# The closing sums of the modulation groups traced with a lower priority

## The chip, the cores and the metric

The kernel runs on one core of a Trainium2 chip. The metric is the device time of one execution in microseconds (us). Before the change three runs took 2878.17, 2879.86 and 2882.39 us, the median is 2879.86 us.

## The reference

The reference computes two layers of a backbone over 512 latent and 256 context tokens of width 1024, in float32. Each layer has a SwiGLU feed-forward half step (ffn1), a mixer of four head groups, and a second half step (ffn2). What the change touches is only the modulations: nine vectors of 1024 numbers for each layer, for the latent tokens (from c) and for the context tokens (from c_ctx), which shift and scale the inputs of each step and gate its output.

```
def ada_mods(s, w, b, dt):
    m = (s @ w.astype(jnp.float32) + b.astype(jnp.float32)).astype(dt)
    m = m.reshape(m.shape[0], N_MOD, D_MODEL)
    return [m[:, k, None, :] for k in range(N_MOD)]

def ffn_half(h, g, w_i, w_o, shift, scale, gate):
    y = modulate(rms_norm(h, g), shift, scale)
    a, b = jnp.split(y @ w_i, 2, axis=-1)
    return h + FFN_RES * gate * ((jax.nn.silu(a) * b) @ w_o)
```

Here s is the SiLU of c or c_ctx (two rows), and w has 1024 rows and 9216 columns for each layer.

## The kernel before

The tokens lie along the free axis, the features on the 128 partitions. A product of float32 operands is made of three TensorE products of parts of 12 bits: a weight tile `wr` from DRAM is split into `wh` (a copy on ACT, L378) and the rest `wl` (a subtraction on DVE, L379), and the input is kept as a pair of such parts, `g`. A column tile of a feed-forward input is 8 row blocks x 3 products x 2 pieces of the tokens (258 and 510 columns, their form is named 128x258 and 128x512), 48 matmuls at L389 into one PSUM tile `pi`. The tiles go in pairs: tile a (for the SiLU), then tile b (the factor). The PSUM pool `psb` that they and the output products `po` share has two buffers, so the next pair's tile a needs the buffer that this pair's tile a leaves. It is left when DVE has copied two shift columns (L448, `bc`) and multiplied the tile by the tokens' norm factors (L449, `z<-pi,R`). For tile b DVE does L453 and L455.

Under these products lies the work of the modulations that later steps need, in `ada_steps`: 32 groups of 512 columns (14 of layer 0 in its ffn1, 9 of layer 1 in layer 0's ffn2, 9 more in layer 1's ffn1). A group has two loads `wa` of 1 MB (L248) and 16 operations of DVE on them (2 at L254, which begin the two sums `acc`, and 14 at L256, which add to them). Then `done()` closes the group: four matmuls by a column of ones add `acc` over the partitions (L263, output `pa`; the profile shows each as two records), ACT copies the sums (`arow`, L265), two transposes (L268, output `pt`) turn them, and DVE adds them and the bias into the modulations (L238). The two `acc` are buffers of the pool `small` under the tag "sq", of which there are two in all: the next group's L254 can begin only when this group's L263 has read its `acc`. In the feed-forward input the loads `wr` and `wa` take turns in the same buffers (tag "wraw").

Each engine executes its own queue in order. The order is set when the program is built: the scheduler of the tile context takes, for each engine, from the instructions whose inputs a simulated time line has ready the one of the highest priority, and the priority is the place in which it was traced, unless the code raises or lowers it (`tc.high_priority(offset)`; a negative offset puts the instructions that many places later). The hooks, among them the two steps of each group, are traced between the column tiles. L1559 and L1564 are matmuls of the S5 coefficients, traced as hooks too; L281 makes a gate from the modulations, L495 adds an output product to the residual; L1438, L1460 to L1462 are DVE operations for S5.

Of the kernel before, what the change touches and what calls it, by code (L numbers as in the profile page):

```python
# [30 lines left out]
FINAL_AT = 2  # L31
SUMS_AT = 1


class Net:
# [63 lines left out]
    def setup_rest(self):  # L99
        """what the first tiles' first products don't need"""  # L100
        nc = self.nc
        for f in self.ada_first(0, 4, "l" * 12 + "z" * 4):
            f()
        for j in range(NT):
            self.hg_shift(j, 0, 0)
        self.rms_factor(TT)
        self.load_rpb()
        self.load_vectors(0, self.REST)
        for part in (self.FIRST, self.REST):
            self.load_vectors(1, part)  # L110
        for t, s in ((self.cos, "k_cos"), (self.sin, "k_sin"), (self.perm, "k_perm"), (self.bones, "k_bones")):
            nc.sync.dma_start(t, self.A[s])

    def load_rpb(self):
        """the neighbourhood's biases with something to read before and after them"""
        nc = self.nc
        m = 2 * 4 * 15 * 31
        self.rpb = self.dram.tile([m + 128], F32, name="rpb")
        z = self.const.tile([1, 64], F32, name="zrow")
        nc.vector.memset(z, 0.0)  # L120
        nc.sync.dma_start(self.rpb[0:64].unsqueeze(0), z)
        nc.sync.dma_start(self.rpb[64 + m:128 + m].unsqueeze(0), z)
        nc.sync.dma_start(self.rpb[64:64 + m].unsqueeze(0), self.A["na_rpb"].rearrange("l h a b -> (l h a b)").unsqueeze(0))
# [5 lines left out]
    def load_vectors(self, l, names=None):  # L129
        """rows to columns; of a layer's rows the first ones or those after them"""  # L130
        nc, A = self.nc, self.A
        pk = self.small.tile([P, TT], F32, name=self.nm("pack"), tag="sq", bufs=2)[:, :P]
        if l < 2:
            q = nc.scalar if l == 0 and names == self.FIRST else nc.sync
# [29 lines left out]
    def load_rows(self, t, b):  # L164
        """128 tokens' half"""
        raw = self.t("g")
        src = self.A["x"][0, t * P:(t + 1) * P, :] if t < 4 else self.A["ctx"][0, (t - 4) * P:(t - 3) * P, :]
        self.nc.sync.dma_start(raw[:, :512], src[:, b * 512:(b + 1) * 512])
        return raw
# [14 lines left out]
    def park(self):  # L184
        """the residual, to DRAM"""
        self.hd = self.dram.tile([NT, P, TT], F32, name=self.nm("hd"))
        for j in range(NT):
            self.nc.sync.dma_start(self.hd[j], self.h[j][:, :TT])
# [6 lines left out]
    def ada_first(self, q0, groups, tags):  # L195
        """two loads of 512 columns of the first layer's modulations, from 512 * q0 on, and products on TensorE, `groups`
        of them at a time: closures for two row blocks each, loads and products on their own if asked for"""
# [34 lines left out]
    def ada_add(self, l, c, parts):  # L232
        """parts, [128, q, b, r], and the bias"""
# [6 lines left out]
    def ada_steps(self, l, q, ring=None):  # L240
        """two closures for 512 columns of a layer's modulations: products on VectorE, their sum over the partitions on
        TensorE"""
# [3 lines left out]
        def rows(k0):  # L246
# [10 lines left out]
            if k0:  # L257
                done()
# [35 lines left out]
    def hg_tile(self, j, l, mi, gs, nt):  # L294
        """`mi` None: the shifts come later, and the squares are there"""
# [23 lines left out]
    def exp_small(self, pool, out, x):  # L319
        """exp of a few numbers, to float32's accuracy, on VectorE"""  # L320
# [16 lines left out]
    def rsqrt(self, r, src, scale):  # L337
        """(src * scale + eps) ** -0.5 of a few numbers: a guess from the exponent, three steps of Newton's"""
# [56 lines left out]
    def in_tile(self, w, nt):  # L395
        """[128, 1024]: columns 254, 255 the shifts' products, from 256 on the tokens'"""
        ps = self.psb.tile([P, 1024], F32, name=self.nm("pi"), tag="psb")
        self.mm(self.in_chunks(ps, nt), w, self.hgx, NT)
        return ps
# [4 lines left out]
    def in_pair(self, wa, wb, nt, late):  # L404
        """two of them; what needs the shifts, made by `late`, comes last"""
# [9 lines left out]
    def ffn(self, l, w_in, w_out, gate, nt, finish, hooks=(), late=None, ring=None):  # L415
        """`gate` is called when it is first needed; `hooks` are traced one list by one between the column tiles;
        `late` is called before the first product that needs the shifts,
        `ring` is for the output's weights if given"""
# [102 lines left out]
    def split_kept(self, raw, kn, j):  # L521
        """the two parts of a column tile's weights, to be kept"""
# [38 lines left out]
    def sums(self, hf, c):  # L561
        """tokens' factors; the second half's last squares come on their own"""
# [34 lines left out]
class Mixer:  # L597
    """One layer's four head groups. Tokens: latent 0..511, context 512..767."""
# [40 lines left out]
    def scratch(self, name):  # L639
        """a pool for what comes next in the place of the last one"""  # L640
# [6 lines left out]
    # column tile, whether it has the context's tokens in any case, where it goes, order of tokens  # L647
# [4 lines left out]
    def beside(self):  # L652
        """what is traced after which column tile"""
# [13 lines left out]
    def evac(self, ps, nt, tag, way):  # L667
        """tokens * R + bias; the latent ones column by column if `way` says so"""
# [16 lines left out]
    def split(self, src, nt, tag="l", slow=False):  # L685
        """a high part and what is left"""
# [10 lines left out]
    def lru(self):  # L697
        """states of both directions, added; the gates' sigmoids as 0.5 + 0.5 tanh(x / 2)"""
# [70 lines left out]
    def softplus_neg(self, o, lam):  # L769
        """8 * softplus(-lam), [128, 4]"""  # L770
# [25 lines left out]
    def softmax(self, p, s, acc, bias=None, r=-1.0):  # L796
        """exp(x - max) and its sums; r * (s + bias) is -x"""
# [7 lines left out]
    def transposed(self, dst, blocks, scalar):  # L805
        """128-column blocks, transposed, side by side in dst"""
# [7 lines left out]
    def attention(self):  # L814
        """all units, each one's stages one after the other's; a group's operands are made ahead of it"""
# [20 lines left out]
    def group(self, units, done):  # L836
        """units in pairs of heads; `done` with (o, factors), [64 of two heads, queries] in PSUM, behind the last; a
        unit: scores, probabilities' parts to multiply with what"""
# [35 lines left out]
    def factors(self, sm, m):  # L874
        """1 / sums [queries, m] as [64 of two heads, queries]"""
# [10 lines left out]
    def ctx_units(self, qs, ks, vs, y, r=lambda qi, hh: -1.0):  # L886
        """two heads' context queries over the context's keys"""
# [16 lines left out]
    def gqa_norm(self):  # L904
        """each token's factors of its two heads, the queries', negative, for the scores; v token by token"""
# [27 lines left out]
    def gqa_scale(self):  # L933
        """the keys' factors"""
# [8 lines left out]
    def gqa_turn(self):  # L943
        """positions' rotations"""
# [9 lines left out]
    def stack_q(self, src, nt, scale=1.0, tag="g"):  # L954
        """[hi; lo] of each of a tile's two heads"""
# [10 lines left out]
    def stack_k(self, src, hh, tag="g"):  # L966
        """[hi; hi] and [lo; lo] of one of a tile's two heads"""
# [9 lines left out]
    def stack_ks(self, src):  # L977
        """the same of both heads"""
# [49 lines left out]
    def na_gather(self, head):  # L1028
        """[queries (c, r), (row, column) of keys in a band] of the head's biases"""
# [8 lines left out]
    def na_bias(self, gs, v):  # L1038
        """two heads' masked biases [queries (c, r), keys (c, r)], and zeros for the context's keys"""
# [67 lines left out]
    def s5_in(self):  # L1107
        """u as [group, h, 7 - s, chunk], chunks ctx | lat | ctx, in DRAM"""
# [134 lines left out]
def mixed(units, more):  # L1243
    """pairs of `more` behind some pairs of the units"""
# [11 lines left out]
def by_columns(ap, way):  # L1256
    """[128, row, column] of tokens that lie column by column, from the first on or from the last"""
# [4 lines left out]
def tables():  # L1262
    """what depends on shapes alone"""
# [36 lines left out]
class S5Coef:  # L1300
    """Coefficients of a layer's S5 scans in chunks of 8 tokens, parked in DRAM.
    [128 (re|im, state), 32 (direction, group)] throughout, but for the tables of rotations:
    [128 (direction, state), 16 groups, 95]."""

    def __init__(self, net, l):
# [3 lines left out]
        # by (direction, pair of groups): the two products' weights; cos, sin, decay  # L1309
# [5 lines left out]
    def steps(self):  # L1315
        """closures, traced one after the other; pools open with the first and close with the last"""
# [28 lines left out]
    def base(self):  # L1345
# [39 lines left out]
        # (a - 1) / lambda  # L1385
# [18 lines left out]
        # powers 0..8 of a; the imaginary parts as [-; +]  # L1404
# [22 lines left out]
    def load(self, d):  # L1427
        """one direction's b, [re; im] and [im; re], and c; the skip's weights, as diagonals"""
# [18 lines left out]
    def bc(self, d):  # L1447
        """one direction's b and c with the discretization's factor and with signs"""
# [22 lines left out]
    def tables(self):  # L1471
        """cos and sin of the chunks' angles, by doubling"""
# [22 lines left out]
        for g in range(0, 16, 4):  # L1495
# [4 lines left out]
            m = 1  # L1500
# [23 lines left out]
    def weights(self, g0):  # L1524
        """two groups of one direction"""
# [47 lines left out]
    def toeplitz(self):  # L1573
        """[group, h, (t - s + 7, h')] of both directions"""
# [19 lines left out]
def spread(hooks, steps, first=0):  # L1594
    """evenly over the column tiles from the `first` on, but the last of each group"""
# [71 lines left out]
```

## Time and profile before

| | before |
|---|---|
| runs, us | 2878.17, 2879.86, 2882.39 (median 2879.86) |
| span of the profiled execution | 2877.7 us |
| TensorE busy | 2819.1 us (98%) |
| VectorE busy | 1742.3 us (61%) |
| ScalarE busy | 906.5 us (32%) |
| GpSimd busy | 757.7 us (26%) |
| DVE on L256, 448 instructions | 358.6 us, 849 ns each |

The profile gives the span of the profiled execution, from its first to its last instruction; the median of the runs is 2.2 us longer, which is taken for what lies around the span. A row of a time line is a start, a duration, the engine, the source line, the operation with output and inputs by the program's names, and in brackets how long the engine stood idle before it and what it waited for. Rows with x2 or x4 put several instructions together.

### The profile page before, as it was taken

How to read it: one execution, taken by the hardware profiler on the slowest of the kernel's cores; microseconds unless marked ns; L12 is line 12 of the kernel's file. 1: busy time of each engine (PE TensorE's matmuls, PEld its weight loads, DVE VectorE, ACT ScalarE, POOL GpSimd, SP SyncE). 2: the span in 40 equal slices, each digit the busy share in tenths (PEclk: the TensorE clock that was granted, in tenths of full speed). 3: DMA queues.
4: the chain of work that ended last, by engine and by line, in shares of the span. 5: the costliest groups of instructions: out<-in, count | busy, mean ns of one | idle time of the engine just before them, and what ended most of it. 6: DMA issues, size and time to landing. Idle time of an engine off the chain costs nothing.

```text
span 2877.7 us, 43478 instructions
## 1 busy us (share of the span) xinstructions
PE 2819.1 (98%) x17293; PEld 2437.7 (85%) x17293; DVE 1742.3 (61%) x3178; ACT 906.5 (32%) x1478; POOL 757.7 (26%) x957
## 2 busy tenths in 40 slices
PE   7999999999999999999999999999999999999998
PEld 4888888888877888888888888888888887899998
DVE  6868577676857566363634766465466876444445
ACT  4212121235546422112123321222224645322223
POOL 2822233221323311000001176332312434201001
PEclk9999999999999999999999999999999999999999
DMA  6445324353323333222311335233254343232231
GB/s 227 134 108 167 112 96 141 123 185 118 115 62 74 103 115 99 87 96 95 107 54 54 118 101 142 80 123 106 74 168 145 118 106 89 79 96 83 88 96 52
DMA packets 295901, 312.13 MB, mean 108 GB/s; under 512 B 58991, under 2 KB 243202, under 8 KB 295698
## 3 DMA queue, kind: packets, MB, share of 16 engines
q1 hardware_dynamic: 266990, 293.97, 31.8%
q0 software_dynamic: 5664, 12.59, 1.9%
q10 hardware_dynamic: 23044, 2.78, 0.7%
q8 instruction: 137, 2.24, 0.3%
q14 instruction: 66, 0.54, 0.1%
HBM read 276.09 MB, written 29.02 MB: 106 GB/s over the span
## 4 chain that ended last, share of the span: by engine, by line
PE 88%; DVE 6%; DMA 2%; ACT 2%; issue 1%; POOL 0%; SPq 0%; ACTq 0%; DVEq 0%; POOLq 0%
PE pi L389 51%; PE po L389 23%; PE po L1236 4%; DVE acc L256 2%; PE po L862 2%; PE pt L810 2%; DMA wa<-in_w_ada_dram 1%; PE ps L793 1%; PE pa L263 1%; DVE wl L379 1%; PE ps L794 1%; DMA l<-in_w_ada_dram 1%; PE pl L734 1%; DVE z L455 0%; PE pa L215 0%
## 5 line engine op out<-in xcount | busy, mean ns | idle before, releaser
L389 PE MATMUL pi<-g,wh 128*128 128x258 f32 (+2 forms) x6656 | 1408.7, 330 | 8.4 <-ACT wh L378 2.6
L389 PEld LDWEIGHTS pi<-g,wh 128*128 128x128 f32 x6656 | 1101.4, 191 | 132.2 <-issue 15.0
L389 PE MATMUL pi<-g,wl 128*128 128x258 f32 (+2 forms) x3328 | 828.1, 329 | 0.7 <-DVE wl L379 0.7
L378 ACT CAST wh<-wr 128x1024 fp32r<-128x1024 f32 (+3 forms) x380 | 338.2, 890 | 1397.4 <-PE pi L389 674.8
L389 PEld LDWEIGHTS pi<-g,wl 128*128 128x128 f32 x3328 | 607.4, 191 | 60.6 <-issue 2.5
L389 PE MATMUL po<-l,wh 128*128 128x512 f32 (+1 forms) x2464 | 566.1, 344 | 0.9 <-DVE e L495 0.8
L389 PEld LDWEIGHTS po<-l,wh 128*128 128x128 f32 x2464 | 387.9, 188 | 63.9 <-issue 3.9
L459 POOL TENSOR_TENSOR l<-z,l 128x768 fp32r<-128x768 f32 (+1 forms) x88 | 159.1, 1808 | 1061.4 <-ACT l L458 955.4
L379 DVE TENSOR_TENSOR wl<-wr,wh 128x1024 fp32r<-128x1024 f32 (+3 forms) x380 | 407.0, 1071 | 50.3 <-ACT wh L378 47.5
L256 DVE SCALAR_TENSOR_TENSOR acc<-wa,s,acc 128x512 f32<-128x512 f32 x448 | 358.6, 849 | 39.4 <-DMA wa<-in_w_ada_dram 38.6
L495 DVE SCALAR_TENSOR_TENSOR e<-po,gt,e 128x512 f32<-128x512 f32 (+1 forms) x296 | 176.2, 631 | 307.4 <-PE po L389 250.7
L389 PE MATMUL po<-l,wl 128*128 128x512 f32 (+1 forms) x1232 | 337.5, 343 | 1.0 <-DVE wl L379 1.0
L453 DVE TENSOR_TENSOR z<-pi,R 128x768 f32<-128x768 f32 (+2 forms) x91 | 78.4, 865 | 301.3 <-PE pi L389 301.3
L389 PEld LDWEIGHTS po<-l,wl 128*128 128x128 f32 x1232 | 194.5, 188 | 32.6 <-DVE wl L379 2.0
L448 DVE COPY bc<-pi 128x2 f32<-128x2 f32 x88 | 13.7, 156 | 189.4 <-PE pi L389 189.4
L458 ACT CAST l<-z 128x768 fp32r<-128x768 f32 (+1 forms) x88 | 68.8, 782 | 160.5 <-DVE z L455 160.5
L1545 POOL TENSOR_TENSOR ww<-AR,BB 128x256 f32<-128x256 f32 x32 | 25.9, 808 | 341.4 <-PE pw L1564 309.5
L455 DVE SCALAR_TENSOR_TENSOR z<-z,pi,z 128x512 f32<-128x512 f32 (+1 forms) x154 | 107.1, 730 | 5.5 <-ACT z L451 0.7
L317 POOL TENSOR_TENSOR ssq<-ssq,sq 128x768 f32<-128x768 f32 (+1 forms) x35 | 67.5, 1929 | 161.0 <-ACT sq L316 161.0
L451 ACT ACTIVATE z<-z,bc 128x512 f32<-128x512 f32 (+1 forms) x154 | 90.0, 625 | 62.7 <-DVE z L449 51.3
L449 DVE TENSOR_TENSOR z<-pi,R 128x768 f32<-128x768 f32 (+1 forms) x88 | 77.5, 880 | 3.7 <-ACT R L366 3.7
L1236 PE MATMUL po<-l,wh 128*128 128x512 f32 (+1 forms) x264 | 71.9, 356 | 0.0
(349 smaller groups left out, 2632.0 us busy)
## 6 DMA issues: line engine op xcount, KB each, us to landing
wr<-in_w_ffn_in_dram SPq DMA_DIRECT2D x88, 1024.0 KB
wa<-in_w_ada_dram SPq DMA_DIRECT2D x64, 1024.0 KB
wr<-in_w_ffn_out_dram SPq DMA_DIRECT2D x48, 512.0 KB
wr<-in_w_ffn_out_dram SPq DMA_DIRECT2D x32, 640.0 KB
wr<-in_w_in_dram SPq DMA_DIRECT2D x16, 1024.0 KB
W<-s5w SPq DMA_DIRECT2D x32, 256.0 KB
wr<-in_w_out_dram SPq DMA_DIRECT2D x8, 1024.0 KB
l<-in_w_ada_dram SPq DMA_DIRECT2D x24, 256.0 KB
```

Source lines behind the costliest of these rows:

```text
L256: nc.vector.scalar_tensor_tensor(acc[r], raw[:, k], s, acc[r], ALU.mult, ALU.add)
L378: nc.scalar.copy(hi[:, :kn], raw[:, :, o:o + P])
L379: nc.vector.tensor_sub(lo[:, :kn], raw[:, :, o:o + P], hi[:, :kn].bitcast(F32))
L389: nc.tensor.matmul(dst, lhsT=wt[:, k, :], rhs=xt[:, a:b], start=(k == 0 and i == 0), stop=(k == kn - 1 and i == 2))
L449: nc.vector.tensor_mul(ta[:, :nt], pa[:, 256:256 + nt], self.R[:, :nt])
L451: nc.scalar.activation(ta[:, a:b], ta[:, a:b], AF.Silu, bias=bc[:, i:i + 1])
L453: nc.vector.tensor_mul(tb[:, a:b], p, self.R[:, a:b])
L455: nc.vector.scalar_tensor_tensor(tb[:, a:b], tb[:, a:b], pb[:, 254 + i:255 + i], ta[:, a:b], ALU.add, ALU.mult)
L458: nc.scalar.copy(uh[:, :nt], tb[:, :nt])
L459: nc.gpsimd.tensor_sub(ul[:, :nt], tb[:, :nt], uh[:, :nt].bitcast(F32))
L495: self.nc.vector.scalar_tensor_tensor(self.h[j][:, a:b], ps[:, a:b], gate[:, j, i:i + 1], self.h[j][:, a:b], ALU.mult, ALU.add)
L1236: self.nc.tensor.matmul(dst, lhsT=wt[:, k, :], rhs=xt[:, a:b], start=(c == 0 and i == 0), stop=(c == NT - 1 and i == 2))
```

## The change

`done()`, the part that closes a group, is traced with a priority 150 places lower. Nothing else is computed in another way; the numbers of instructions are the same on every engine. (The rest of the diff empties comments.)

```
+CLOSING = 150
@@ in ada_steps, rows(k0)
             if k0:
-                done()
+                with self.tc.high_priority(offset=-CLOSING):
+                    done()
```

Lines of the changed kernel stand one or two further down: L254 becomes L255, L256 L257, L263 L265, L268 L270, L238 L239, L379 L381, L389 L391, L449 L451, L453 L455, L455 L457, L448 L450, L1559 L1561, L1564 L1566, L1567 L1569.

The first place is in layer 0's ffn2, TensorE's queue at the closing `pa_1553` with its transposes `pt_1555`. Before, it stands between the tiles of a pair: behind tile b of the pair that has just ended (`pi_1543`) and ahead of the next tile a (`pi_1560`), whose PSUM buffer is long free.

```order
L389 MATMUL pi_1543_9876<-g_1514_9647,wh_1541_9872 128x258
L389 MATMUL pi_1543_9876<-g_1514_9647,wh_1541_9872 128x512
L263 MATMUL pa_1553_9961<-acc_1550_9941,ones_80 32x256 x2
L263 MATMUL pa_1553_9961<-acc_1551_9943,ones_80 32x256 x2
L389 MATMUL pi_1560_9980<-g_1464_9168,wh_1558_9976 128x258
L389 MATMUL pi_1560_9980<-g_1464_9168,wh_1558_9976 128x512
```

Now it stands one pair later: `pi_1560` (tile a) and `pi_1563` (tile b) are ahead of it, and `pi_1574`, the next tile a, behind it.

```order
L391 MATMUL pi_1563_10033<-g_1514_9647,wh_1561_10029 128x258
L391 MATMUL pi_1563_10033<-g_1514_9647,wh_1561_10029 128x512
L265 MATMUL pa_1553_9961<-acc_1550_9941,ones_80 32x256 x2
L265 MATMUL pa_1553_9961<-acc_1551_9943,ones_80 32x256 x2
L270 MATMUL pt_1555_9968<-ident_78,z_1554_9962 128x128 x2
L391 MATMUL pi_1574_10112<-g_1464_9168,wh_1572_10108 128x258
L391 MATMUL pi_1574_10112<-g_1464_9168,wh_1572_10108 128x512
```

The 96 matmuls of a pair have moved ahead of the closing; the transposes now follow it at once.

On VectorE the same place, before: the next group's sums `acc_1570` and `acc_1571` begin while tile a runs, and the multiplication that frees `pi_1560` comes among the additions.

```order
L379 TENSOR_TENSOR wl_1559_9977<-wr_1556_9972,wh_1558_9976 128x1024
L453 TENSOR_TENSOR z_1546_9927<-pi_1543_9876,R_84 128x768
L254 TENSOR_SCALAR acc_1570_10098<-wa_1569_10096,s2_102 128x512
L254 TENSOR_SCALAR acc_1571_10100<-wa_1569_10096,s2_102 128x512
L455 SCALAR_TENSOR_TENSOR z_1546_9927<-z_1546_9927,pi_1543_9876,z_1545_9926 128x512
L455 SCALAR_TENSOR_TENSOR z_1546_9927<-z_1546_9927,pi_1543_9876,z_1545_9926 128x256
```

And now:

```order
L450 COPY bc_1564_10082<-pi_1560_9980 128x2
L381 TENSOR_TENSOR wl_1573_10109<-wr_1556_9972,wh_1572_10108 128x1024
L255 TENSOR_SCALAR acc_1570_10098<-wa_1569_10096,s2_102 128x512
L451 TENSOR_TENSOR z_1565_10083<-pi_1560_9980,R_84 128x768
L455 TENSOR_TENSOR z_1566_10084<-pi_1563_10033,R_84 128x768
L255 TENSOR_SCALAR acc_1571_10100<-wa_1569_10096,s2_102 128x512
L257 SCALAR_TENSOR_TENSOR acc_1570_10098<-wa_1569_10096,s2_102,acc_1570_10098 128x512
```

The first operation on `acc_1570`, which writes the buffer of `acc_1550` that the closing reads, stands ahead of the L451 that frees the PSUM buffer of `pi_1560`.

The second place is in layer 0's ffn1, where two groups end close together. On TensorE two closings, `pa_598` and `pa_622`, now stand behind one another, ahead of the next tile `pi_644`; before, a whole pair of tiles lay between them.

```order
L265 MATMUL pa_598_4464<-acc_570_4276,ones_80 32x256
L1561 MATMUL pw_606_4492<-ident_78,wr_607_4493 128x128 x2
L1566 MATMUL pw_606_4492<-C1_523_3867,ww0_605_4488 128x16 x2
L265 MATMUL pa_598_4464<-acc_570_4276,ones_80 32x256
L265 MATMUL pa_598_4464<-acc_571_4278,ones_80 32x256 x2
L270 MATMUL pt_600_4471<-ident_78,z_599_4465 128x128 x2
L265 MATMUL pa_622_4639<-acc_602_4477,ones_80 32x256
L1561 MATMUL pw_630_4667<-ident_78,wr_631_4668 128x128 x2
L1566 MATMUL pw_630_4667<-C1_523_3867,ww0_629_4663 128x16 x2
L265 MATMUL pa_622_4639<-acc_602_4477,ones_80 32x256
L391 MATMUL pi_644_4714<-g_61_291,wh_642_4710 128x258
```

The closing `pa_622` reads `acc_602`, the sums of the group whose first operation has to wait for the closing `pa_598`.

## Rows read from the trace of the kernel before

**Rows 1.** The page: busy time of each engine, and the chain that ended last.

```profile
PE 2819.1 (98%) x17293; PEld 2437.7 (85%) x17293; DVE 1742.3 (61%) x3178; ACT 906.5 (32%) x1478; POOL 757.7 (26%) x957
...
PE 88%; DVE 6%; DMA 2%; ACT 2%; issue 1%; POOL 0%; SPq 0%; ACTq 0%; DVEq 0%; POOLq 0%
```

**Rows 2.** Waits of PE: what for, us in total, times, longest.

```profile
PE pa L263 <- DVE acc L256: 4.2, 4, 2.1
...
PE pi L389 <- DVE wl L379: 0.7, 2, 0.5
```

**Rows 3.** Time line of PE around one closing in ffn2 of layer 0.

```profile
1057.66 0.51 PE L389 MATMUL pi<-g,wh 128*128 128x258 f32 x2
1058.10 0.64 PE L263 MATMUL pa<-acc,ones 128*32 128x256 f32 x8
1058.67 0.62 PE L389 MATMUL pi<-g,wh 128*128 128x258 f32 x2
1059.13 0.51 PE L389 MATMUL pi<-g,wl 128*128 128x258 f32 x2
...
1062.67 0.52 PE L389 MATMUL pi<-g,wh 128*128 128x258 f32 x2
1063.03 0.38 PE L268 MATMUL pt<-ident,z 128*128 128x128 f32 x2
1063.17 0.60 PE L389 MATMUL pi<-g,wh 128*128 128x258 f32 x2
1063.60 0.52 PE L389 MATMUL pi<-g,wl 128*128 128x258 f32 x2
```

**Rows 4.** Time line of DVE at the same place.

```profile
1059.08 0.87 DVE L254 TENSOR_SCALAR acc<-wa,s 128x512 f32<-128x512 f32 x2
...
1069.10 0.94 DVE L449 TENSOR_TENSOR z<-pi,R 128x768 f32<-128x768 f32 x1
```

**Rows 5.** A tile that waited for its PSUM buffer: DVE's row.

```profile
148.45 1.48 DVE L455 SCALAR_TENSOR_TENSOR z<-z,pi,z 128x512 f32<-128x512 f32 x2
```

**Rows 6.** The same, PE's row.

```profile
150.08 0.59 PE L389 MATMUL pi<-g,wh 128*128 128x258 f32 x2 [0.38 <-DVE z L455]
```

**Rows 7.** Time line of DVE near 1780 us, in ffn1 of layer 1.

```profile
1779.38 2.08 DVE L256 SCALAR_TENSOR_TENSOR acc<-wa,s,acc 128x512 f32<-128x512 f32 x3 [4.35 <-DMA wa<-in_w_ada_dram]
1781.37 0.42 DVE L1460 TENSOR_TENSOR BB<-B,frz 128x256 f32<-128x256 f32 x1
```

**Rows 8.** DVE by line and form, 200 to 640 us: busy, mean ns, idle before.

```profile
L256 DVE SCALAR_TENSOR_TENSOR acc<-wa,s,acc 128x512 f32<-128x512 f32 x168 | 136.2, 865 | 15.2 <-DMA wa<-in_w_ada_dram 15.2
...
L254 DVE TENSOR_SCALAR acc<-wa,s 128x512 f32<-128x512 f32 x24 | 17.6, 772 | 0.5 <-PE pa L263 0.3
...
L453 DVE TENSOR_TENSOR z<-pi,R 128x768 f32<-128x768 f32 x16 | 15.3, 954 | 37.2 <-PE pi L389 37.2
```

**Rows 9.** Time line of PE at the second place of the order.

```profile
488.09 0.62 PE L263 MATMUL pa<-acc,ones 128*32 128x256 f32 x4 [1.48 <-DVE acc L256]
...
488.90 0.62 PE L263 MATMUL pa<-acc,ones 128*32 128x256 f32 x4
...
491.13 0.87 PE L389 MATMUL pi<-g,wh 128*128 128x258 f32 x4
...
506.68 1.07 PE L263 MATMUL pa<-acc,ones 128*32 128x256 f32 x4 [2.09 <-DVE acc L256]
```

**Rows 10.** Stretches: us, busy PE, PEld, DVE, ACT, POOL; PEclk, DMA share, GB/s.

```profile
200.00:297.00 97.00, 97.00 (x561) 81.19 (x560) 75.20 (x110) 21.35 (x31) 27.14 (x27) 1.00 0.42 139
...
504.60:510.10 5.50, 3.42 (x15) 1.61 (x15) 5.50 (x9) 1.86 (x4) 0.00 (x0) 0.69 0.45 133
510.10:513.50 3.40, 3.40 (x12) 2.92 (x13) 3.40 (x5) 0.38 (x1) 2.88 (x4) 0.50 0.60 207
513.50:517.00 3.50, 3.50 (x23) 3.06 (x21) 2.04 (x4) 2.19 (x4) 1.46 (x2) 1.00 0.13 45
```

**Rows 11.** Waits of SP's DMA queue for buffers: us in total, times, longest.

```profile
SPq L248 <- DVE acc L256: 224.9, 33, 25.2
...
SPq L371 <- DVE acc L256: 81.1, 16, 17.3
```

## The prediction

> **What bounds the kernel now.** I read the busy times and the chain that ended last first: TensorE is busy for 98% of the span and is 88% of the chain, VectorE 6% [rows 1]. So anything that makes TensorE stand still is paid in full, and what VectorE does beside it costs nothing as long as it is in time. Then TensorE's waits: for the sums that a closing reads it stands 4.2 us in all, in four waits, and for late weight parts 0.7 us [rows 2]. That is the whole sum that lies open to a later closing. Then the time line around one closing, for its price, and the order of the two queues at the same place, for who waits for whom.
>
> **What a closing costs TensorE today.** It stands between two tiles. From 1057.66 to 1059.13 four matmuls of a tile and the eight records of the closing take 1.47 us; four such matmuls take 0.71 us elsewhere, so a closing costs about 0.75 us, of which 0.57 (1058.10 to 1058.67) is its own. The transposes, inside a tile, cost 0.2 us (four matmuls and they take 0.93 from 1062.67 to 1063.60) [rows 3]. These are paid after the change too, at other places.
>
> **What the change moves.** Of the 32 closings some 25 stand elsewhere in TensorE's queue, most of them the 96 matmuls of one pair later, at the boundary to the next pair, with their transposes right behind them. The DVE work of the following group moves little. Its first operation must wait for the closing that reads the same buffer, and in the new order it stands on VectorE ahead of the L451 that frees the PSUM buffer of the pair's tile a (the pieces of order show it for `acc_1570` and `pi_1560`). Before, that multiplication ran while tile b was computed (1069.10, while tile b ran to 1076) [rows 4]. Now it comes behind the closing, and the next tile a needs its buffer. So at such a boundary there is a chain through both engines: closing, L255, L451, next tile.
>
> **Price of a simple boundary.** First half of the closing, to the end of its last matmul: 0.4 us (half of 0.57 and the drain of 0.64 - 0.57) [rows 3]. Release to VectorE 0.1, an estimate from the next release. L255 0.48 us (0.87 for two that overlap a little) and L451 0.94 [rows 4]. Release of TensorE 0.15 us: L455 ended at 148.45 + 1.48 = 149.93, the tile that waited for it began at 150.08 [rows 5, 6]. Sum 2.07 us from the closing's start to the next tile's. Before it was 0.57, and the transposes' 0.2 now fits into the wait. So each boundary costs 2.07 - 0.57 - 0.2 = **1.3 us**. Its bounds: 0, if the multiplication is already done, and 2.1, if nothing is hidden. I count ten of these, in layer 0's ffn1 (one, near 141 us), ffn2 of layer 0 and ffn1 of layer 1: 13 us. At five of them S5 matmuls stand between the halves of the closing, which delays L255 behind them; from 488.09 to 488.90 one such took 0.81 in place of 0.29 [rows 9]: 5 x 0.5 = 2.5. **Together 16 us.**
>
> **Three boundaries with more ahead of the multiplication.** Near 1780 us the new order has, between the closing and the L451, two L255, six L257 and five S5 operations. With L256 at 0.7 us there (2.08 for three) and the small ones at 0.34 (start to start, 1781.37 to 1781.71) [rows 7] that is 1.0 + 4.2 + 1.7 + 0.94 us, and 0.7 for closing and releases, 8.5 in all against 0.8: +8. Near 1817 the closing has two copies of S5's and a weight part ahead of L451: +3, from the same rows. Near 165 the closing stands ahead of the output product for which the gate L283 is still to be made from it: sums, copy, transposes, L239, L283, then the first residual add: +2. **Together 13 us**, bounds 4 (three simple prices) and 20.
>
> **Layer 0's ffn1, 200 to 640 us.** Here VectorE has little to spare: 75.2 us of 97 busy [rows 10]. Eleven boundaries at 1.3 are 14 us. At the second place of the order two closings stand behind one another, and TensorE waits for a whole group: two L255 at 0.77, fourteen L257 at 0.865, and L451, L455 and the tile's two L457 between them, 0.95 + 0.95 + 1.5, is 1.5 + 12.1 + 3.4 = 17 us [rows 8], the L457 as the two L455 of before [rows 5]. The waits that it replaces were 1.48 and 2.09 us [rows 9]: +13. That the two closings' matmuls lie within it is already in the 0.57 above. Then lateness: VectorE stands at L255 until a closing that comes later, and what it does not do meanwhile is pushed to where weight parts are due. The bounds are 0 (it fits into the 21.8 us that VectorE idles in those 97) and 22 (all of it is lost once over). Today TensorE waits 0.7 us in all for weight parts [rows 2], which speaks for the lower half: I take 9. **Together 36 us**, bounds 14 and 55.
>
> **The clock.** After the wait of 2.09 us the granted clock fell: 0.69 in the stretch with the wait, 0.50 (1.2 GHz) from 510.10 to 513.50, where 12 matmul records took 3.40 us; at 1.00 (2.4 GHz) 23 took 3.50 [rows 10]. So the fall cost 3.40 - 12 x 3.50/23 = 1.6 us. After the wait of 1.48 us it did not fall: L389 x4 took 0.87 us at 491.13 [rows 9]. A simple boundary's idle time is 2.07 - 0.57 = 1.5 us, on the side of the row without a fall. I count ten places with waits of 2 us or more (the three with more ahead, six or seven in layer 0's ffn1): 10 x 1.6 = **16 us**, bounds 0 and 25 x 1.6 = 40.
>
> The Trainium skill's page "TensorE: Matmul & The Clock Gate", section "Part 1: The HAM clock gate (the "warmup" mystery)", speaks against the change: it says that half rate is the default and that only sustained activity releases it, so idleness that the change adds would be paid twice. The fall at 510.10 agrees; the wait of 1.48 us shows that not every pause is punished. By the rule alone, with a fall at all 25 places, this term would be 40 us in place of 16.
>
> **The sum.** 16 + 13 + 36 + 16 = 81; the 4.2 us of today's waits go with it, 3.6 of them are taken off in the second place and the rest is lost in rounding. 2877.7 + 81 = 2959 us of span; the median of the runs lies 2.2 above the span, so about **2960 us**, +2.8%. Loads: the buffer that wr and wa share is held longer where a group begins later, and SP's queue waits 225 and 81 us for those sums already [rows 11]; without a stall of TensorE on a load in today's trace from this, I cost it at nothing, its cover being the 18 us of a tile, and leave it to the upper end.
>
> **The rivals.**
> (1) Faster. The closings no longer interrupt a running tile or wait for their sums: 4.2 us of waits and, at best, the 0.2 of each of 25 transposes go, 2877.7 - 4.2 - 5 + 2.2 = 2871 us. It holds if L451 is done before tile b ends, that is if L255 stood behind it or its buffer were free. For it: the waits exist [rows 2]. Against: the order puts L255 ahead, and the buffer is one of two. Chance 0.05.
> (2) No change: closings that are moved by a pair find the multiplication mostly done and cancel the waits, 2878 to 2882 us. It needs the same release as (1) at most places. Chance 0.04.
> (3) Only the boundary's price: nothing late in layer 0, no fall of the clock: 25 x 1.3 = 33, less 4, +29: 2909 us. For it: the slack of 21.8 us and the wait of 1.48 us without a fall [rows 9, 10]. Against: the back-to-back closings, which must wait for the whole group whatever the slack. Chance 0.14.
> (4) More: the clock falls at most boundaries (+40 in place of 16), lateness doubles, and loads come late: 2877.7 + 16 + 13 + 55 + 40 + 2 = about 3004 us. For it: the fall after 2.09 us [rows 10] and SP's long waits for sums [rows 11]. Chance 0.12.
> (5) The forecast, 2960 us, own range 2930 to 2985. Chance 0.65.
>
> A measurement of this kernel can tell about 0.2% (6 us) from no change. Only (1) lies below, (2) within: faster 0.05, same 0.04, slower 0.91. The range from 2905 to 3005 takes in (3), (5) and most of (4).
>
> **What would show it.** Right: new rows "L391 waits for DVE z L451" of 1.5 to 2 us at the boundaries, some 20 of them; one long wait of about 17 us near 510 us, at L265, for L257; a granted clock below 1.00 in stretches of layer 0's ffn1 and behind 1780 us; idle time of DVE's L255 for PE's pa of many us where it was 0.3 [rows 8]. Wrong: if those L391 rows begin without a wait, the order was misread, and the time stays; if the waits are there but the clock stays at 1.00, 16 us are too many; if L391 waits for wl L381 more than 20 us in all, lateness was sized too low.

## The result, and the profile after

The changed kernel takes 2965.17 us (median of four runs, 2963.44 to 2967.40), the kernel before 2880.45 us in the same comparison: a ratio of 1.0296, 95% interval 1.0281 to 1.0311. The forecast was 2960 us, with a range of 2905 to 3005. The span of the profiled execution is 2962.4 us, 84.7 more than before, with the same number of instructions on each engine. The page's busy times (engine, us, share of the span, instructions), to compare with [rows 1]:

```profile
PE 2849.5 (96%) x17293; PEld 2454.8 (83%) x17293; DVE 1731.1 (58%) x3178; ACT 909.5 (31%) x1478; POOL 740.2 (25%) x957
```

TensorE was busy for 30 us more though it does the same (some 17 us of it are the clock, below), and stood still for 54 us more (2962.4 - 2849.5 against 2877.7 - 2819.1). What it waited for, in us, times and the longest one, answers to [rows 2]:

```profile
PE pa L265 <- DVE acc L257: 24.8, 4, 14.1
PE pi L391 <- DVE z L451: 17.5, 17, 6.6
PE pt L270 <- ACT z L267: 11.9, 20, 0.9
...
PE po L391 <- ACT wh L380: 4.9, 2, 3.4
...
PE pi L391 <- DVE wl L381: 0.7, 2, 0.5
```

The first was 4.2 us; the second, the third and the fourth were not there; the last has not changed. The wait of VectorE for a closing at a group's first operation, 0.3 us between 200 and 640 us before [rows 8], is now, over the whole span:

```profile
DVE acc L255 <- PE pa L265: 94.1, 17, 8.0
```

A simple boundary, at the first place of the order (layer 0's ffn2). TensorE's time line answers to [rows 3]:

```profile
1128.37 0.64 PE L265 MATMUL pa<-acc,ones 128*32 128x256 f32 x8
1129.85 0.44 PE L270 MATMUL pt<-ident,z 128*128 128x128 f32 x2 [0.84 <-ACT z L267]
1130.55 0.59 PE L391 MATMUL pi<-g,wh 128*128 128x258 f32 x2 [0.26 <-DVE z L451]
```

And VectorE's, which answers to [rows 4]:

```profile
1121.10 1.23 DVE L381 TENSOR_TENSOR wl<-wr,wh 128x1024 fp32r<-128x1024 f32 x1 [0.98 <-ACT wh L380]
1129.05 0.49 DVE L255 TENSOR_SCALAR acc<-wa,s 128x512 f32<-128x512 f32 x1 [6.72 <-PE pa L265]
1129.45 0.95 DVE L451 TENSOR_TENSOR z<-pi,R 128x768 f32<-128x768 f32 x1
1130.32 0.95 DVE L455 TENSOR_TENSOR z<-pi,R 128x768 f32<-128x768 f32 x1
```

VectorE stood for 6.72 us at L255 while L451, whose input had long been there (L450 had copied from the same tile at 1119.96), stood behind. From the closing's start to the next tile's it is 1130.55 - 1128.37 = 2.18 us; 2.07 were predicted. A part of the wait is put down to the transposes, since they stand ahead of the tile and wait for ACT's copy; the tile waits for L451 after that.

The same boundary with more ahead of L451, near 1780 us of before. TensorE:

```profile
1841.48 0.64 PE L265 MATMUL pa<-acc,ones 128*32 128x256 f32 x8
1842.64 0.44 PE L270 MATMUL pt<-ident,z 128*128 128x128 f32 x2 [0.52 <-ACT z L267]
1849.69 0.98 PE L391 MATMUL pi<-g,wh 128*128 128x258 f32 x2 [6.61 <-DVE z L451]
```

It is 8.2 us from closing to tile (8.5 predicted). The rows of VectorE between, first and last:

```profile
1842.16 0.88 DVE L255 TENSOR_SCALAR acc<-wa,s 128x512 f32<-128x512 f32 x2 [6.75 <-PE pa L265]
...
1848.61 0.94 DVE L451 TENSOR_TENSOR z<-pi,R 128x768 f32<-128x768 f32 x1
```

The two closings behind one another (near 548 us), where the second stands ahead of the end of its own sums, and two more places of this kind that the prediction did not see (near 256 and 306 us). TensorE there:

```profile
256.40 1.07 PE L265 MATMUL pa<-acc,ones 128*32 128x256 f32 x4 [3.86 <-DVE acc L257]
257.78 1.01 PE L391 MATMUL pi<-g,wh 128*128 128x258 f32 x2 [0.32 <-ACT wh L380]
...
305.87 1.06 PE L265 MATMUL pa<-acc,ones 128*32 128x256 f32 x2 [6.05 <-DVE acc L257]
...
547.87 1.03 PE L265 MATMUL pa<-acc,ones 128*32 128x256 f32 x2 [14.10 <-DVE acc L257]
```

VectorE before 548 us: the group that could not begin before the closing ahead of it, and runs while TensorE stands.

```profile
532.85 1.35 DVE L255 TENSOR_SCALAR acc<-wa,s 128x512 f32<-128x512 f32 x2 [2.69 <-PE pa L265]
...
538.82 9.57 DVE L257 SCALAR_TENSOR_TENSOR acc<-wa,s,acc 128x512 f32<-128x512 f32 x12
```

At the gate, near 165 us, TensorE waits first for a weight part and then for the residual that the gate scales:

```profile
166.63 0.61 PE L391 MATMUL po<-l,wh 128*128 128x512 f32 x2 [1.54 <-ACT wh L380]
...
176.08 0.62 PE L391 MATMUL po<-l,wh 128*128 128x512 f32 x2 [1.65 <-DVE e L497]
```

Near 669 us a load came late: first ScalarE's row, which copies the weight part, then TensorE's.

```profile
668.19 1.14 ACT L380 CAST wh<-wr 128x512 fp32r<-128x512 f32 x2 [3.23 <-DMA wr<-in_w_ffn_out_dram]
```

```profile
668.86 0.71 PE L391 MATMUL po<-l,wh 128*128 128x512 f32 x2 [3.41 <-ACT wh L380]
```

The clock, as in [rows 10] (us; PE, PEld, DVE, ACT, POOL busy; then the granted clock, DMA share, GB/s). Nine stretches of the feed-forward steps at half clock, where there was one:

```profile
167.50:170.90 3.40, 3.39 (x11) 2.91 (x12) 1.23 (x1) 0.00 (x0) 0.55 (x1) 0.50 0.92 200
256.20:263.10 6.90, 5.91 (x20) 3.43 (x21) 5.21 (x9) 3.38 (x5) 0.00 (x0) 0.51 0.60 172
304.00:314.30 10.30, 8.43 (x26) 5.15 (x27) 5.59 (x8) 3.42 (x6) 4.33 (x6) 0.50 0.43 145
536.10:556.60 20.50, 8.73 (x27) 5.37 (x28) 18.78 (x25) 4.09 (x8) 7.40 (x9) 0.50 0.38 122
645.40:648.80 3.40, 3.40 (x12) 2.88 (x11) 3.40 (x7) 0.29 (x1) 0.00 (x0) 0.51 0.44 87
669.20:672.70 3.50, 3.48 (x11) 2.67 (x10) 3.50 (x7) 1.95 (x4) 0.00 (x0) 0.51 1.06 369
1747.90:1751.30 3.40, 3.40 (x12) 2.93 (x11) 3.40 (x5) 0.00 (x0) 3.09 (x5) 0.50 0.04 8
1846.80:1853.70 6.90, 4.01 (x13) 3.46 (x14) 6.90 (x13) 1.43 (x3) 1.31 (x2) 0.51 0.87 189
1891.20:1894.60 3.40, 3.06 (x10) 2.69 (x11) 3.40 (x6) 1.12 (x2) 3.17 (x5) 0.50 0.29 78
sum 61.70, PE 43.81 PEld 31.49 DVE 51.40 ACT 15.69 POOL 19.84; mean PE 4.87 PEld 3.50 DVE 5.71 ACT 1.74 POOL 2.20
```

TensorE was busy for 43.8 us in them. With the prediction's own rate (1.6 of 3.4 us lost) that is 20.6 us, less the 3.2 of the one stretch before, some 17. One of them came behind a simple boundary:

```profile
1744.80 0.44 PE L270 MATMUL pt<-ident,z 128*128 128x128 f32 x2 [0.90 <-ACT z L267]
1746.56 0.59 PE L391 MATMUL pi<-g,wh 128*128 128x258 f32 x2 [1.32 <-DVE z L451]
```

Where the 85 us came from, by the start of the same column tiles in both traces (after minus before, worked out tile by tile), beside the terms of the forecast, its ten falls of the clock put where it counted them:

| stretch of before, us | measured | forecast for it |
|---|---|---|
| to 211 (the first simple boundary, the gate) | +4.9 | 1.3 + 2 + 1.6 = 5 |
| 211 to 651 (layer 0's ffn1) | +47.1 | 36 + 7 x 1.6 = 47 |
| 651 to 1060 (mixer) | +0.2 | 0 |
| 1060 to 1630 (layer 0's ffn2) | +3.6 | 3 x 1.3 = 4 |
| 1630 to 2164 (layer 1's ffn1) | +27.5 | 6 x 1.3 + 2.5 + 8 + 3 + 2 x 1.6 = 25 |
| from 2164 on | +1.3 | 0 |

### The profile page after: what moved, and what is told of

Its sections match the earlier page's. It is cut to its first block, busy times and chain, and to the rows that moved or that the text cites. A ratio compares the mean times of both kernels' runs of the same rounds, so it can differ in the third digit from the quotient of the medians.

```text
span 2962.4 us, 43464 instructions
## 1 busy us (share of the span) xinstructions
PE 2849.5 (96%) x17293; PEld 2454.8 (83%) x17293; DVE 1731.1 (58%) x3178; ACT 909.5 (31%) x1478; POOL 740.2 (25%) x957
## 5 line engine op out<-in xcount | busy, mean ns | idle before, releaser
L391 PE MATMUL pi<-g,wh 128*128 128x258 f32 (+2 forms) x6656 | 1412.1, 331 | 22.5 <-DVE z L451 17.5
L391 PEld LDWEIGHTS pi<-g,wh 128*128 128x128 f32 x6656 | 1109.3, 193 | 148.0 <-issue 13.3
L391 PE MATMUL pi<-g,wl 128*128 128x258 f32 (+2 forms) x3328 | 830.4, 330 | 0.7 <-DVE wl L381 0.7
L380 ACT CAST wh<-wr 128x1024 fp32r<-128x1024 f32 (+3 forms) x380 | 337.8, 890 | 1465.8 <-PE pi L391 732.8
L391 PEld LDWEIGHTS pi<-g,wl 128*128 128x128 f32 x3328 | 611.0, 192 | 62.7 <-issue 3.1
L391 PE MATMUL po<-l,wh 128*128 128x512 f32 (+1 forms) x2464 | 569.0, 344 | 7.2 <-ACT wh L380 4.9
L381 DVE TENSOR_TENSOR wl<-wr,wh 128x1024 fp32r<-128x1024 f32 (+3 forms) x380 | 402.6, 1060 | 87.0 <-ACT wh L380 83.3
L391 PEld LDWEIGHTS po<-l,wh 128*128 128x128 f32 x2464 | 389.8, 189 | 70.3 <-ACT wh L380 6.8
L257 DVE SCALAR_TENSOR_TENSOR acc<-wa,s,acc 128x512 f32<-128x512 f32 x448 | 353.5, 833 | 10.4 <-DMA wa<-in_w_ada_dram 9.6
L391 PE MATMUL po<-l,wl 128*128 128x512 f32 (+1 forms) x1232 | 338.6, 344 | 0.3 <-DVE wl L381 0.3
L391 PEld LDWEIGHTS po<-l,wl 128*128 128x128 f32 x1232 | 195.4, 189 | 31.2 <-DVE wl L381 1.5
L455 DVE TENSOR_TENSOR z<-pi,R 128x768 f32<-128x768 f32 (+2 forms) x91 | 78.3, 863 | 242.8 <-PE pi L391 242.8
L450 DVE COPY bc<-pi 128x2 f32<-128x2 f32 x88 | 13.8, 157 | 232.5 <-PE pi L391 232.4
L453 ACT ACTIVATE z<-z,bc 128x512 f32<-128x512 f32 (+1 forms) x154 | 90.1, 625 | 56.5 <-DVE z L451 53.2
L457 DVE SCALAR_TENSOR_TENSOR z<-z,pi,z 128x512 f32<-128x512 f32 (+1 forms) x154 | 102.0, 695 | 5.4 <-ACT z L453 0.8
L255 DVE TENSOR_SCALAR acc<-wa,s 128x512 f32<-128x512 f32 x64 | 35.0, 566 | 96.1 <-PE pa L265 94.1
L451 DVE TENSOR_TENSOR z<-pi,R 128x768 f32<-128x768 f32 (+1 forms) x88 | 77.5, 881 | 3.7 <-ACT R L368 3.7
```

The source lines that it names most:

```text
L257: nc.vector.scalar_tensor_tensor(acc[r], raw[:, k], s, acc[r], ALU.mult, ALU.add)
L380: nc.scalar.copy(hi[:, :kn], raw[:, :, o:o + P])
L381: nc.vector.tensor_sub(lo[:, :kn], raw[:, :, o:o + P], hi[:, :kn].bitcast(F32))
L391: nc.tensor.matmul(dst, lhsT=wt[:, k, :], rhs=xt[:, a:b], start=(k == 0 and i == 0), stop=(k == kn - 1 and i == 2))
L451: nc.vector.tensor_mul(ta[:, :nt], pa[:, 256:256 + nt], self.R[:, :nt])
L453: nc.scalar.activation(ta[:, a:b], ta[:, a:b], AF.Silu, bias=bc[:, i:i + 1])
```

## The experiments

**One part alone: transposes and addition late.** The sums and the copy keep their place.

```
     def done():                                # called without high_priority
         ... four matmuls, nc.scalar.copy(arow, ps)
+        with self.tc.high_priority(offset=-CLOSING):
             pt = ...; two transposes; self.ada_add(...)
```

> Half of the change: the four sums and the copy into arow at their old priority, the transposes and the addition of the bias 150 places lower. Theory A: arow gets its buffer in time, nothing is held back, 2875 to 2890 us. Rival (the transposes' wait for ACT's copy, 11.9 us in 20 waits after the change, is a cost of its own): about 2892 us. Rival B' (any part of the closing at a pair's boundary costs): 2920 us or more.

Measured: 2879.56 us, ratio 0.9995 (0.9986 to 1.0004). No change. What costs is the late sums with their copy, not the late turning alone. ACT's copy is early in this run, so it doesn't price the 11.9 us that TensorE waited for late copies. That these are for the most part inside the boundary's wait is read from the rows above: the transposes begin at 1129.85, L451 ends at 1130.40 and the tile, which needs it, begins at 1130.55.

**Is it the priority that puts L255 ahead of L451?**

```
-            nc.vector.tensor_copy(bc, ...); nc.vector.tensor_mul(ta, ...)
+            with tc.high_priority(offset=200):
+                nc.vector.tensor_copy(bc, ...); nc.vector.tensor_mul(ta, ...)
```

> The changed kernel, with the two DVE operations that free tile a's PSUM buffer (L450, L451) traced with a priority 200 places higher. Theory A: the priority doesn't matter, since L451 can't be placed before arow has its buffer in the ring; 2955 to 2975 us, waits for z L451 as in the changed kernel. Rival B (L255 stands ahead because of the order of priorities): L451 comes ahead, the boundary's 1.3 us go, 2925 to 2940 us.

Measured: 2960.23 us, ratio 1.0278 (1.0264 to 1.0292). TensorE's waits (the lines have moved by one or two):

```profile
PE pa L266 <- DVE acc L258: 24.6, 4, 14.2
PE pi L392 <- DVE z L453: 17.8, 17, 6.6
```

They are those of the changed kernel. A priority 200 places higher does not place the multiplication earlier, so it was not a matter of rank; the argument from it is that something that it needs was not to be had before the closing.

**The copied sums out of the ring of z.** `arow`, ACT's copy of the sums, takes one of the five buffers z, as ta and tb of every pair do. First it was put into the unused columns of the second acc buffer:

```
-            ps, arow = self.bank("pa")[:, :256], self.t("z")[:, :256]
+            ps, arow = self.bank("pa")[:, :256], acc[1][:, 512:768]
```

> The changed kernel (CLOSING = 150), but the copied sums arow stand in the unused last 256 columns of the group's second acc buffer, not in one of the five buffers z that the tiles' ta and tb take in turn. Theory A (arow's place in the ring of z holds back ta's multiplication L451, and with it the PSUM buffer of the next tile): L451 no longer waits for the closing, the waits of TensorE at the boundaries (17.5 us for z L451, 24.8 for acc) go to under 6 us together, the time is 2870 to 2890 us. Rival B (the prediction's reading: L255, which waits for the closing, is the cause whatever arow does): the waits stay, about 2965 us. Rival C (a late closing itself costs, by its matmuls at the boundary): about 2920 us.

> The kernel before with arow in the second acc buffer and no lowered priority. It is the control of the run above: what the new place of arow does alone. Theory A: arow never held L449 long there, 2875 to 2885 us. Rival: the next group's second L254 now waits for the transposes, 10 us slower, about 2890 us.

Measured: 2955.75 us, ratio 1.0258 (1.0244 to 1.0272), and the control 2906.16 us, 1.0090 (1.0076 to 1.0103). The waits for z L451 were gone altogether, so that part of theory A held; but the waits for acc were still 20.8 us and the time hardly fell. As all the reason, theory A is refuted. The control, slower than both of its expectations, shows that the place itself costs 25 us (an acc buffer is now held until the transposes, which is the likely reason), so it was done again with a buffer that nobody else uses:

```
+            arow = self.own.tile([P, 256], F32, tag="ar", bufs=1)   # a pool around each ffn
```

> CLOSING = 150, and arow in a buffer of its own (1 KB for each partition, in a pool around each feed-forward step), so that it takes no turn in the ring of z; the acc buffers are as before, two. Theory A2 (two rings hold the work back: z by arow, which costs the simple boundaries, and acc, which costs layer 0's ffn1): the waits for z L451 (17.5 us) are gone, those for acc (24.8) stay, 2915 to 2940 us. Rival A1 (z's ring alone): 2875 to 2890 us. Rival D (acc's ring alone, z's costs nothing): 2950 to 2965 us.

> The control: arow in its own buffer, closings at their old priority. All theories: arow had no share in the old order, 2874 to 2884 us. A time above 2890 would mean that the new pool itself costs.

Measured: 2949.74 us, ratio 1.0243 (1.0227 to 1.0258); the control 2884.58 us, 1.0019 (1.0009 to 1.0028). TensorE's waits with CLOSING = 150:

```profile
PE pa L265 <- DVE acc L257: 22.0, 3, 13.5
PE pi L391 <- ACT wh L380: 8.2, 2, 5.6
PE po L391 <- ACT wh L380: 5.7, 1, 5.7
```

No wait for z L451 is left: ring z is what held L451 back. The time lies at the end of rival D all the same, and the 2915 to 2940 us of theory A2 were missed. A new cost had come in: without the block at the boundaries the four sums go one by one between a tile's matmuls. The time that the sums occupied TensorE (busy, mean ns of one, idle before), for this kernel:

```profile
L265 PE MATMUL pa<-acc,ones 128*32 128x256 f32 x256 | 49.6, 414 | 22.0 <-DVE acc L257 22.0
```

It was 28.4 us in the control. In the order the 128 sums stand in 74 blocks here, in 45 in the control, in 44 before the change and in 51 after it. So of the 65 us over the control some 21 are the sums' row, 18 waits for acc (3.5 us in the control), 11 late wh; for the rest there is the clock, which was at half rate for 51 us between 175 and 671 us and nowhere in the control's feed-forward steps. This experiment doesn't give ring z's price by itself.

**A third buffer in the ring of acc**, added to the kernel above (for the room, three small buffers of gains and norm factors are given up):

```
+            n-th buffer: every third one from the new pool ([P, 512], tag "acc", bufs=1), else tag "sq", bufs=2
```

> The kernel with arow in its own buffer and CLOSING = 150, and a third buffer in the ring of acc (a group needs two, so that the next group can begin one of its two sums without the closing; three small buffers of norm factors are given up for the room). Theory A2 (acc's ring is what is left): TensorE's waits for acc go from about 25 to under 15 us, the time is 10 to 30 us below that of arow_own. Rival E (the closings cost where they stand, whatever the buffers): no change against arow_own.

Measured: 2931.57 us, ratio 1.0186 (1.0169 to 1.0203), 18 us below. The waits for acc fell by 19.3 us, to this:

```profile
PE pa L269 <- DVE acc L261: 2.7, 3, 1.2
```

Theory A2, as expected; rival E falls. Against the gain stand 13.3 us that TensorE now waits at L1565 for S5 operands, where it waited 2.9 us at this step in the kernel above.

**Acc's ring without its hold.** On top of arow in its own buffer, both sums of a group go into one buffer, so the ring of two holds two groups (the two rows of modulations are not kept apart, so the values are others; the work is the same).

```
-                        acc.append(self.small.tile(...))
+                        acc.append(acc[0] if r else self.small.tile(...))
```

> CLOSING = 150 with arow in its own buffer, and the two sums of a group put into one buffer, one after the other by the same 16 operations (the sums of the two rows of modulations are so not kept apart, the values are others; the amount of work is the same). A group then needs one of the two acc buffers, and the next group can begin before the closing. Theory A2 (what is left with arow apart is acc's ring): the waits for acc fall from 22 us to under 6, the time to 2875 to 2900 us, within 15 us of its control. Rival E (the closings cost where they stand, or VectorE's load is the cause): 2935 to 2950 us, as with two buffers.

> The control of the run above: the two sums of a group in one buffer, arow in its own, closings at their old priority. Theory A2: 2875 to 2890 us, a few us below the kernel with two buffers (2884.6), since TensorE's waits for acc (3.5 us) go.

Measured: 2897.99 us, ratio 1.0060 (1.0044 to 1.0077), and the control 2888.99 us, 1.0028 (1.0017 to 1.0039). With the same VectorE work and the same lowered priority the loss over the control is 9 us, where it was 65 with the ring closed and 85 in the changed kernel. The 9 us are the least of it: the control lost time of its own (4.9 us of waits for wl, falls of the clock near 277 and 1785 us), and over the kernel before it is 18 us. TensorE did not wait once for acc, and VectorE's wait at L255 for a closing is 9.7 us in place of 94.1. The sums, scattered here too, took this, against 22.5 us in the control:

```profile
L265 PE MATMUL pa<-acc,ones 128*32 128x256 f32 x256 | 41.8, 391 | 0.0
```

**Other offsets.**

```
-CLOSING = 150
+CLOSING = 100      (and 50, and -50)
```

> The changed kernel with CLOSING = 100 in place of 150: in its order 10 groups' L255 stand ahead of the freeing L451, of 21 with 150 and 2 before. Theory A (each such place has its price): about 8/19 of the 85 us, 2905 to 2925 us. Rival F (any lowering moves the closings and costs): 2945 us or more. Rival G (the cost comes only from the pairs of closings behind one another): 2880 to 2895 us.

> The changed kernel with CLOSING = 50. In its order 2 groups' L255 stand ahead of the freeing L451, as before the change, and 17 closings at a tile's boundary. Theory A2: with 100, 85% of the loss was there at 10 such places, so the count of places doesn't give the size, but without held-back buffers there is none: 2876 to 2890 us. Rival H (the loss grows with the offset in proportion): about 2905 us.

> The priority of the closings raised by 50 places (CLOSING = -50) in place of lowered. Theory A2: both rings get their buffers back sooner; TensorE's waits for acc (4.2 us before) may grow, since a closing now can stand ahead of its sums' end: 2872 to 2888 us. Rival I (the old order was at an optimum and any move costs): 2890 us or more.

Measured: 2952.70 us (1.0255, 1.0240 to 1.0271), 2914.80 us (1.0119, 1.0104 to 1.0134) and 2916.88 us (1.0126, 1.0111 to 1.0141). All three expectations of theories A and A2 missed. With 100, 73 us go although TensorE waits only 5.3 us for acc and 6.1 us for z L451: the row of its sums grew to 53.1 us, and late weight parts (L391 for wh L380) cost 13.0 us, one of 8.6 us among them. So the two rings are not the whole price of a late closing there. With 50, and with the priority raised, TensorE waits 1.0 and 1.3 us for acc and not for z L451, and still 35 and 37 us go. The sums' rows tell where, for CLOSING = 50:

```profile
L265 PE MATMUL pa<-acc,ones 128*32 128x256 f32 x256 | 53.1, 398 | 1.0 <-DVE acc L257 1.0
```

and for -50:

```profile
L265 PE MATMUL pa<-acc,ones 128*32 128x256 f32 x256 | 58.3, 391 | 1.3 <-DVE acc L257 1.3
```

Before they took 28.7 us: 24 and 30 us of the loss stand in this one row. The sums lie in 84 and 94 blocks, so a block takes 0.63 and 0.62 us, and 0.65 before (28.7 us in 44). A time line of one such closing (-50):

```profile
1641.52 0.62 PE L265 MATMUL pa<-acc,ones 128*32 128x256 f32 x2
1642.06 0.50 PE L391 MATMUL pi<-g,wh 128*128 128x512 f32 x1
1642.49 0.62 PE L265 MATMUL pa<-acc,ones 128*32 128x256 f32 x2
1643.04 0.39 PE L391 MATMUL pi<-g,wl 128*128 128x258 f32 x1
1643.35 0.62 PE L265 MATMUL pa<-acc,ones 128*32 128x256 f32 x2
1643.90 0.50 PE L391 MATMUL pi<-g,wl 128*128 128x512 f32 x1
1644.33 0.62 PE L265 MATMUL pa<-acc,ones 128*32 128x256 f32 x2
1644.88 0.98 PE L391 MATMUL pi<-g,wh 128*128 128x258 f32 x4
```

From 1641.52 to 1644.88 it is 3.36 us for four sums and three of the tile's matmuls (0.18 each elsewhere), so 2.8 us for a closing that took 0.57 to 0.75 in one block [rows 3]. Two records alone are busy for 0.62 us, all eight in one block for 0.64. No version that ran is faster than the kernel before.

## Why the prediction was right

- **The chain at the boundary** was the mechanism, and its size was right: 2.18 us where 2.07 were worked out, 1.3 us net each. The tiles' starts in ffn2 of layer 0, where nothing else happens, moved by 3.6 us for three boundaries. What the sum left out is that the transposes wait there for ACT's copy (0.84 us); it lies beside L255 and L451 and so cost nothing more.
- **Why L451 stands behind L255** the prediction took from the order without a reason. The runs give one. A closing that is traced later also asks later for its buffer z, `arow`, and ta, whose turn in the ring comes behind it, is not placed before that: a higher priority of ta didn't help, and with another buffer for arow, in two kernels, all 17.5 us of those waits were gone. So the closing, which should have given way to the tile, held the tile up. That it moves to the pair's boundary fits this: there TensorE has no tile left that it may begin. The turn in the ring as the reason, and this last part, are argued from the order and from these runs; no run shows the turns themselves.
- **The places with more ahead**: +8 was right (8.2 us from closing to tile, 8.5 predicted). The gate, with the boundary before it, came to the 5 us of the forecast with one fall of the clock, but in other pieces: 1.65 us of wait for the residual, and 1.54 us for a weight part that the prediction did not name (0.95 us of such a wait stood there before; that the closing delayed it is not shown). The place near 1817 came to 5.6 us with the clock, against 3 and a fall.
- **Layer 0's ffn1**: 47 us with the clock, as forecast, but its terms missed and made up for one another, which is luck. The waits for acc grew by 20.6 us, not by 13: at the doubled closing it was 14.1 us, not 17, but three more closings stand ahead of the end of their own sums, with 3.86, 6.05 and 0.84 us. Eleven simple boundaries were forecast at 14 us; TensorE waited for L451 at six, and all its waits at boundaries there (L451, the transposes, an operand of S5) are 9.2 us. "Lateness", 9 us for weight parts, was mis-sized: the waits for wl stayed at 0.7 us, and 3.7 us came for wh. Of these, 3.41 us were a late load (ACT waited 3.23 us for wr), and loads the prediction had put at nothing. The reason for the waits for acc is the second ring: a group can't begin while acc is held, so VectorE lay idle (94.1 us at L255) and then had the group to do while TensorE stood. Ring3 and the run with one buffer for both sums show it. The bounds of 14 to 55 us covered the sum; its own terms give 27 to 49.
- **The clock**: 16 us forecast from ten falls; nine came, and some 17 us more than before by the windows. This too is partly luck, since fewer falls were dearer: 20.6 us for nine is 2.3 us each, where 1.6 was taken. The fall from which the 1.6 was read had lasted longer than the one stretch priced: 0.69 over the 5.50 us ahead of it [rows 10] is another 3.4 us at half clock. The line between 1.48 us (no fall) and 2.09 us [rows 9] was no rule: the clock fell at 1747.9 behind a simple boundary with waits of 0.90 and 1.32 us and at 645.4 behind one with 0.51, 0.53 and 0.49 us, while the same three waits near 512 us, and most other simple boundaries, brought none. The Trainium skill (page "TensorE: Matmul & The Clock Gate", section "Part 1: The HAM clock gate (the "warmup" mystery)") has half rate as the default, which sustained activity releases. The nine falls agree with it; taken for all 25 places it would have given too much.
- **The rivals**: (1) and (2) needed L451 ahead of the closing; the 17 waits for it show the opposite. (3), the boundary's price alone, lacked the waits for acc and the falls of the clock. (4) doubled the lateness and took the clock to fall at most boundaries; one load did come late (3.41 us), and the clock fell at nine places.

## What to carry to other kernels

A lower priority for a piece of work doesn't only put it later: every buffer of a rotating pool that it takes or gives back comes later with it, and work of higher priority that needs the next turn of that ring waits. So before moving a step, list the rings in which it has a turn, and look in the built order for a first writer standing ahead of the instruction that frees a tile. The rings are not everything: with 100 places only 11 us of waits at them were left, and 73 us were lost. So also count in how many blocks the short matmuls stand, and keep those with other weights in one: a closing in four pieces cost about four to five times what it cost in one.

## What the runs showed of the hardware

Sums that stand between a tile's matmuls one by one are far dearer than in a block: 2.8 us against 0.57 to 0.75 us for the same eight records. The price goes by blocks and not by records: a block of two records is busy for 0.62 us and one of eight for 0.64, and the row's busy time is 0.62 to 0.65 us for each block whether there are 44, 84 or 94 of them. Why it is so no run shows. In the rows above each pair of records takes 0.54 us to the next matmul's start, and that single matmul of the tile 0.31 to 0.43 where 0.18 is usual. Over a whole run this was 24 to 30 us, without any wait in the profile: it shows only as busy time of the row.
